# Transformer encoder trunk: the first stage rearranged (small inputs as rows, silu's row in PSUM, latent product behind the chunk loop)

## The chip, the cores and the metric

The kernel runs on one core of a Trainium2 chip. The metric is the device time of one execution in microseconds (us). Five engines work side by side, each through its own queue in order: TensorE (PE; its weight loads, PEld, overlap), VectorE (DVE), ScalarE (ACT), GpSimd (POOL) and SyncE (SP), which issues most DMAs. Operands lie in SBUF, matmul results in the eight banks of PSUM.

## The reference

Two layers of an encoder with hidden width 1024 on 512 positions. `c` goes through silu and one product per layer that gives shift, scale and gate for both halves of the layer.

```python
c_act = jax.nn.silu(c)
for l in range(DEPTH):
    mod = c_act @ w_mod[l] + b_mod[l]
    sh1, sc1, gt1, sh2, sc2, gt2 = jnp.split(mod, 6, axis=-1)
    h = rms_norm(x, g_norm_mix[l]) * (1.0 + sc1[:, None]) + sh1[:, None]
    proj = h @ w_in[l]
    q_d, k_d, v_d, cq, ckv, k_rope = jnp.split(proj, cuts, axis=-1)
    ...
    o_dil = dilated_attention(q_d, k_d, v_d, positions, slopes)
    o_mla = latent_attention(cq, ckv, k_rope, positions, ...)
    x = x + gt1[:, None] * (jnp.concatenate([o_dil, o_mla], -1) @ w_out[l])
    h = rms_norm(x, g_norm_mlp[l]) * (1.0 + sc2[:, None]) + sh2[:, None]
    x = x + gt2[:, None] * (jnp.square(jax.nn.relu(h @ w_mlp_in[l])) @ w_mlp_out[l])
```

The dilated heads subtract a slope times the distance of two positions; the latent heads turn part of q and k by sines and cosines of the positions.

## The kernel before, in words

x lies transposed, as eight tiles of 128 features by 512 positions (`xT`, chunk k or j). Every matrix product is made of three matmuls (`mm3`, lines 238 to 240): operands are split into a rounded part `hi` and the rest `lo`, and hi·hi, lo·hi and hi·lo are added in PSUM. A weight block is loaded as `raw` or `zz`, ACT makes `wh` and POOL makes `wl` (`load_split`, lines 233 and 234).

The first stage, up to the first head of attention, goes like this. Loads: c, the identity, the columns of small parameters (`cols`), positions as columns (`posc`), the rotary frequencies (`inv`), x. Silu of c is spread over all partitions as a row of 1024 (`cb`) by a product of ones with diagonal matrices. The squares of x are added up and summed over the features by a matmul (line 723). Sine and cosine of the angles are made on POOL and ACT (lines 131 to 151), with a table load on ACT ahead and one behind. Then comes the chunk loop (lines 720 to 750), k from -1 to 7: DVE multiplies two blocks of modulation weights (128 x 1024) by `cb` with a running sum (line 170), which gives shift and scale of a chunk; ACT makes `am` and `mod` of them (lines 195 and 194); DVE makes u, x times the inverse norm (lines 738 and 729); ACT makes `hi` and the full u (lines 742 and 743), and `lo` is made by POOL for even and by DVE for odd places (lines 745 and 733). With each chunk PE adds to four banks of the first dilated pair (`PR[0]`, 384 columns) and to four banks of the latent product (`W`, 416 columns).

Behind the loop come the norms of the dilated pair, its tail of 16 transposes (line 469), the norms and tail of the latent product (line 537), and the distances of the positions (`distances`, lines 304 to 325). Then eight head stages `st` follow, four of dilated pairs and four of latent pairs, each woven with the product of the next pair: a score (line 482), on DVE the bias and maximum (line 343), on ACT the exponential, a scaling on ACT or POOL, four transposes (line 358) and the product with the values (line 368).

The order on each engine is set by a scheduler that plays the program through. Instructions that are marked (`keep_in_program_order`, or issued inside `manual_schedule` for the listed engines) stay in the order of the code; the others are put where the scheduler sees room. Each tile name is a ring of buffers (`BUFS`: `qk` and `ot` 8, `raw` 3, `zz` 2, `wh`, `wl` and `mm` 4, `P` 3, `sc` and `tr` 2); a new tile waits until the readers of the one before it in its buffer are done.

Of the kernel before, what the change touches and what calls it, by code (L numbers as in the profile page):

```python
# [16 lines left out]
L = 2  # L17
D = 1024
# [24 lines left out]
def trunk(ctx: ExitStack, tc: tile.TileContext, a):  # L43
# [42 lines left out]
    cs = col(8, "cs")  # L86
    SY.dma_start(cs, a["c"].rearrange("(k p) -> p k", p=128))
    ident = const.tile([128, 128], F32, name="ident")
    SY.dma_start(ident, a["ident"])
    cols = [col(N_COL, f"cols{l}") for l in range(L)]  # L90
    SY.dma_start(cols[0], a["cols"][0])
    posc = const.tile([128, 4], I32, name="posc")
    SY.dma_start(posc, a["pos"].rearrange("(t p) -> p t", p=128))
    inv = col(16, "inv")
    SY.dma_start(inv, bass.AP(tensor=a["inv"].tensor, offset=a["inv"].offset, ap=[[0, 128], [1, 16]]))

    xT = [const.tile([128, S], F32, name=f"x{j}") for j in range(8)]
    for j in range(8):
        SY.dma_start(xT[j], a["xT"][j])
    ones = const.tile([128, 128], F32, name="ones")  # L100
# [3 lines left out]


    e = small(8)
    A.activation(e, cs, AF.Exp, scale=-1.0)
    V.tensor_scalar(e, e, 1.0, None, op0=OP.add)
    V.reciprocal(e, e)
    V.tensor_tensor(cs, cs, e, op=OP.mult)  # L110
    cb = const.tile([128, D], F32, name="cb")
    for i in range(2):
        p = ps("sc", (128, 4, 128))
        dg = s2([128, 4, 128])
        for k in range(4):
# [5 lines left out]
    sq0 = s2(tag="o")
    for j in range(8):
        if j == 0:
            A.activation(sq0, xT[j], AF.Square)
        else:
            sq = s2(tag="P")
            A.activation(sq, xT[j], AF.Square)
            V.tensor_tensor(sq0, sq0, sq, op=OP.add)


    pf = col(4, "pf")
    V.tensor_copy(pf, posc)
    ang, kf, w_ = s2([128, 4, 16]), s2([128, 4, 16]), s2([128, 4, 16], tag="b")
    for t in range(4):
        G.tensor_scalar(ang[:, t], inv, pf[:, t:t + 1], 0.0, op0=OP.mult, op1=OP.add)
    G.tensor_scalar(kf, ang, 1.0 / (2 * math.pi), 12582912.0, op0=OP.mult, op1=OP.add)
    G.tensor_scalar(kf, kf, -12582912.0, 0.0, op0=OP.add, op1=OP.add)
    c1 = 6.28125
    c2 = float(np.float32(np.round((2 * math.pi - c1) * 2.0 ** 20) / 2.0 ** 20))
    c3 = 2 * math.pi - c1 - c2  # L140
    for cc in (c1, c2, c3):
        G.tensor_scalar(w_, kf, -cc, 0.0, op0=OP.mult, op1=OP.add)
        G.tensor_tensor(ang, ang, w_, op=OP.add)
    PI_ = 3.1415925
    G.tensor_scalar(ang, ang, PI_, -PI_, op0=OP.min, op1=OP.max)
    A.activation(kf, ang, AF.Abs)
    G.tensor_scalar(kf, kf, -1.0, math.pi / 2, op0=OP.mult, op1=OP.add)
    sin = const.tile([128, 4, 16], F32, name="sin")
    cos = const.tile([128, 4, 16], F32, name="cos")
    A.activation(sin, ang, AF.Sin)  # L150
    A.activation(cos, kf, AF.Sin)
    pre = A.preload_act_table_set("natural_log_exp_and_others")
    tc.keep_in_program_order(pre)
    ctx.enter_context(tc.issue_after(pre.ins))
# [7 lines left out]
    def mod_block(l, i, tag="raw", pool_=False, pin=False, out=None):  # L162
        out = modc[l][:, i:i + 1] if out is None else out
        w = t4(tag, [128, D], F32)
        SY.dma_start(w, a["wmod"][l, i])
        if pool_:
            G.tensor_tensor(w, w, cb, op=OP.mult)
            A.activation(w, w, AF.Copy, accum_out=out)
        else:
            r = V.scalar_tensor_tensor(w, w, 1.0, cb, op0=OP.mult, op1=OP.mult, accum_out=out)  # L170
            if pin:
                tc.keep_in_program_order(r)
# [17 lines left out]
    mraw = col(16, "mraw")  # L190

    def first_norm(j):

        A.activation(modc[0][:, j:j + 1], mraw[:, j:j + 1], AF.Identity, bias=cols[0][:, C_BMOD + j:C_BMOD + j + 1])
        A.activation(amix[0][:, j:j + 1], mraw[:, 8 + j:9 + j], AF.Identity, bias=gb0[:, j:j + 1],
                     scale=cols[0][:, C_GMIX + j:C_GMIX + j + 1])

# [31 lines left out]
    def load_split(src, n, raw="raw", tags=("wh", "wl")):  # L229
        raw = t4(raw, [128, 1024], F32)[:, :n]  # L230
        hi, lo = t4(tags[0], [128, 1024])[:, :n], t4(tags[1], [128, 1024])[:, :n]
        SY.dma_start(raw, src)
        A.activation(hi, raw, AF.Copy)  # L233
        G.tensor_tensor(lo, raw, f(hi), op=OP.subtract)  # L234
        return hi, lo

    def mm3(out, sh, sl, mh, ml, first, last):
        T.matmul(out, sh, mh, start=first, stop=False)  # L238
# [5 lines left out]
    def inv_rms(p, v, y, t):  # L244

        V.tensor_scalar(v, p, 1.0 / D, EPS, op0=OP.mult, op1=OP.add)
        A.activation(t, v, AF.Ln)
# [3 lines left out]
        V.scalar_tensor_tensor(y, t, 1.5, p, op0=OP.add, op1=OP.mult)  # L251
# [719 lines left out]
```

## Time and profile before

| | |
|---|---|
| three runs | 1353.58, 1353.67, 1356.93 us; median 1353.67 |
| the profiled execution | 1351.23 us |
| its span, first to last instruction | 1349.5 us |
| busy: PE, PEld | 1271.8 us (94%), 1116.2 us (83%) |
| busy: DVE, ACT, POOL | 761.6 (56%), 680.4 (50%), 653.0 us (48%) |
| mean granted clock of TensorE | 0.973 of full speed |

A row of the timeline has the start in us, the busy time, engine, source line, operation, tile written and tiles read; x4 says that four instructions are merged. A bracket at the end gives the idle time of the engine ahead of it and what ended it. A name such as `h` or `mm` is that of the tile, without its buffer number. PEq, SPq and the like are an engine's queue.

### The profile page before, as it was taken

What the parts mean: (1) busy time and instruction counts of PE and PEld (TensorE: products, weight loads), DVE (VectorE), ACT (ScalarE), POOL (GpSimd) and SP (SyncE); (2) the same over time, 40 slices, a digit from 0 to 9 for tenths busy, and PEclk for the clock granted to TensorE, in tenths of its full rate; (3) what the DMA queues carried; (4) which work ended last, traced back from release to release, by engine and by line L of the source; (5) the groups of instructions that cost most, each with busy time, mean ns of one, the idle gap of its engine ahead of it and who ended that gap; (6) DMA issues with size and microseconds to landing.
All of it is one profiled execution on the core that took longest, in us unless ns stands there. A gap on an engine that the chain in (4) does not pass through costs nothing.

```text
span 1349.5 us, 19637 instructions
## 1 busy us (share of the span) xinstructions
PE 1271.8 (94%) x7114; PEld 1116.2 (83%) x7114; DVE 761.6 (56%) x1644; ACT 680.4 (50%) x1421; POOL 653.0 (48%) x504
## 2 busy tenths in 40 slices
PE   4889989898999999999999999899799999999999
PEld 2778867777998888888899999798699888888888
DVE  6777787875763561834576678987573122121123
ACT  5567898776542332322247677887653232232321
POOL 5636786674445444444438333545443444444441
PEclk6979989999999999999999999999999999999999
DMA  9335543341244572754534243211111322233221
GB/s 343 113 102 173 182 155 103 105 134 62 71 164 165 185 266 94 266 172 157 167 122 129 79 136 123 85 48 63 60 51 54 103 94 94 94 99 104 94 94 63
DMA packets 57248, 167.62 MB, mean 124 GB/s; under 512 B 8640, under 2 KB 10816, under 8 KB 57152
## 3 DMA queue, kind: packets, MB, share of 16 engines
q1 hardware_dynamic: 57152, 166.38, 37.5%
q8 instruction: 56, 0.92, 0.3%
q14 instruction: 40, 0.33, 0.1%
HBM read 155.87 MB, written 10.49 MB: 123 GB/s over the span
## 4 chain that ended last, share of the span: by engine, by line
PE 66%; POOL 2%; DVE 2%; ACT 2%; issue 2%; DMA 1%; POOLq 0%; DVEq 0%; ACTq 0%
PE mm L240 20%; PE mm L238 20%; PE mm L239 20%; PE tr L368 2%; PE tr L358 1%; POOL wl L234 1%; PE sc L238 1%; PE sc L239 1%; PE sc L240 1%; POOL pt L234 1%; PE sc L482 0%; PE mm L469 0%; DVE pt L362 0%; PE sc L483 0%; PE mm L626 0%
## 5 line engine op out<-in xcount | busy, mean ns | idle before, releaser
L234 POOL TENSOR_TENSOR wl<-raw,wh 128x1024 fp32r<-128x1024 f32 (+3 forms) x174 | 395.7, 2276 | 440.1 <-ACT wh L233 436.4
L233 ACT ACTIVATE wh<-raw 128x1024 fp32r<-128x1024 f32 (+3 forms) x174 | 174.6, 1004 | 263.9 <-PE mm L240 211.7
L659 DVE SCALAR_TENSOR_TENSOR x<-mm,mod,x 128x512 f32<-128x512 f32 (+1 forms) x152 | 92.4, 620 | 255.7 <-PE mm L240 255.2
L238 PE MATMUL mm<-h,wh 128*128 128x512 f32 (+1 forms) x544 | 198.5, 365 | 0.2
L239 PE MATMUL mm<-h,wl 128*128 128x512 f32 (+1 forms) x544 | 198.1, 364 | 0.0
L240 PE MATMUL mm<-h,wh 128*128 128x512 f32 (+1 forms) x544 | 197.9, 364 | 0.0
L238 PE MATMUL mm<-ot,wh 128*128 128x512 f32 (+1 forms) x416 | 147.9, 357 | 7.3 <-ACT ot L651 5.2
L843 ACT ACTIVATE P<-mm 128x512 f32<-128x512 f32 (+1 forms) x80 | 41.1, 513 | 214.3 <-PE mm L240 208.2
L239 PE MATMUL mm<-ot,wl 128*128 128x512 f32 (+1 forms) x416 | 146.7, 354 | 0.0
L240 PE MATMUL mm<-ot,wh 128*128 128x512 f32 (+1 forms) x416 | 144.2, 354 | 2.2 <-POOL ot L652 2.2
L844 DVE SCALAR_TENSOR_TENSOR mm<-mm,P 128x512 f32<-128x512 f32 (+1 forms) x80 | 46.9, 589 | 132.1 <-ACT P L843 132.1
L238 PEld LDWEIGHTS mm<-h,wh 128*128 128x128 f32 x544 | 102.6, 189 | 16.8 <-DVE qk L846 0.6
L239 PEld LDWEIGHTS mm<-h,wl 128*128 128x128 f32 x544 | 102.7, 189 | 16.1
L240 PEld LDWEIGHTS mm<-h,wh 128*128 128x128 f32 x544 | 102.6, 189 | 16.2
L238 PE MATMUL mm<-qk,wh 128*128 128x512 f32 (+1 forms) x288 | 105.3, 366 | 1.0 <-DVE x L659 1.0
L239 PE MATMUL mm<-qk,wl 128*128 128x512 f32 (+1 forms) x288 | 105.3, 365 | 0.0
L240 PE MATMUL mm<-qk,wh 128*128 128x512 f32 (+1 forms) x288 | 105.2, 365 | 0.0
L170 DVE SCALAR_TENSOR_TENSOR pt<-pt,cb 128x1024 f32<-128x1024 f32 x56 | 100.6, 1828 | 0.0
L355 POOL TENSOR_SCALAR P<-P,hs 128x512 f32<-128x512 f32 x64 | 48.4, 756 | 106.0 <-DVE hs L348 85.2
L362 DVE TENSOR_TENSOR pt<-tr,pt 128x512 fp32r<-128x512 f32 x128 | 86.6, 683 | 19.1 <-ACT pt L361 18.5
L238 PEld LDWEIGHTS mm<-ot,wh 128*128 128x128 f32 x416 | 80.1, 193 | 19.2 <-ACT ot L651 5.7
L238 PE MATMUL mm<-wh,h 128*128 128x384 f32 x240 | 81.0, 352 | 11.8 <-ACT h L742 9.8
(290 smaller groups left out, 2980.2 us busy)
## 6 DMA issues: line engine op xcount, KB each, us to landing
raw<-in_w_dram SPq DMA_DIRECT2D x64, 512.0 KB, 3.4
pt<-in_wmod_dram SPq DMA_DIRECT2D x56, 512.0 KB, 4.8
raw<-in_w2a_dram SPq DMA_DIRECT2D x48, 512.0 KB, 3.5
raw<-in_wmod_dram SPq DMA_DIRECT2D x24, 512.0 KB, 3.6
raw<-in_win_dram SPq DMA_DIRECT2D x30, 384.0 KB, 3.1
bias<-b SPq DMA_DIRECT2D x32, 256.0 KB, 2.3
raw<-in_wout_dram SPq DMA_DIRECT2D x16, 512.0 KB, 3.7
raw<-in_w2b_dram SPq DMA_DIRECT2D x16, 512.0 KB, 3.4
```

The costliest lines, as they stand in the source:

```text
L170: r = V.scalar_tensor_tensor(w, w, 1.0, cb, op0=OP.mult, op1=OP.mult, accum_out=out)
L233: A.activation(hi, raw, AF.Copy)
L234: G.tensor_tensor(lo, raw, f(hi), op=OP.subtract)
L238: T.matmul(out, sh, mh, start=first, stop=False)
L239: T.matmul(out, sl, mh, start=False, stop=False)
L240: T.matmul(out, sh, ml, start=False, stop=last)
L355: G.tensor_scalar(P, P, r_, 0.0, op0=OP.mult, op1=OP.add)
L362: V.tensor_tensor(lo, tr, f(hi), op=OP.subtract)
L368: T.matmul(po[:, HALF[qh]], vals(hd, kc), pt[qh][w][:, kc], start=(kc == 0 and w == 0), stop=(kc == 3 and w == 1))
L659: V.scalar_tensor_tensor(xT[j][:, hf], p, gt[:, j:j + 1], xT[j][:, hf], op0=OP.mult, op1=OP.add)
L843: A.activation(r, p, AF.Relu)
L844: V.scalar_tensor_tensor(p, p, 0.0, r, op0=OP.max, op1=OP.mult)
```

## The change

- c and the positions are loaded as rows of contiguous elements and turned into columns by small transposes on PE. Positions, `inv` and `cols` are issued from ACT's queue, so SP has c, the identity and then x.
- Silu's row stays in two PSUM banks (`cbp`); the first 16 modulation products are done in halves of 512 columns against these banks, with two partial sums (`mraw`) that POOL adds (`msum`, `first_sums`). The copy `cb` is made later, for the other modulation blocks.
- All sixteen modulation loads use the eight `qk` buffers. SP loads modulation rows and the dilated weights in turn; the latent weights follow behind.
- The squares are added in a PSUM bank; sine and cosine are one activation, made behind the squares with the table loads around it; the cosine's argument is made on DVE.
- In the chunk loop PE works on the dilated pair only. All `lo` are made by POOL. The latent product follows in two parts of two blocks each, with the dilated tail between them.
- The distances are made on POOL and DVE behind the chunk loop and no longer behind the latent tail; the rope tables move into the second head stage.

The diff, cut to its core (removed lines that the listing above shows are left out):

```diff
...
+    rows = s2([8, 4, 128], tag="b")
+    crow, prow, pi = rows[:, 0], rows[:4, 1].bitcast(I32), rows[:4, 2:].bitcast(I32)
+    SY.dma_start(crow, a["c"].rearrange("(k p) -> k p", k=8))
     SY.dma_start(ident, a["ident"])
...
     for j in range(8):
         SY.dma_start(xT[j], a["xT"][j])
+    A.dma_start(prow, a["pos"].rearrange("(t p) -> t p", t=4))
+    A.dma_start(inv, bass.AP(tensor=a["inv"].tensor, offset=a["inv"].offset, ap=[[0, 128], [1, 16]]))
+    A.dma_start(cols[0], a["cols"][0])
...
+    exp_tables()
     e = small(8)
+    turn = ps("sc")
+    T.transpose(turn[:, :8], crow, ident[:8, :8])
+    A.activation(e, turn[:, :8], AF.Exp, scale=-1.0)
...
+    cbp = [ps("tr") for _ in range(2)]
     for i in range(2):
+        dg = s2([128, 4, 128], tag="P")
...
+        T.matmul(cbp[i], ones, dg.rearrange("p k c -> p (k c)"), start=True, stop=True)
...
+    def first_sums(j):
+        G.tensor_tensor(msum, mraw[:, 0, j:16:8], mraw[:, 1, j:16:8], op=OP.add)
 
     def first_norm(j):
+        A.activation(amix[0][:, j:j + 1], msum[:, 1:2], AF.Identity, bias=gb0[:, j:j + 1],
+                     scale=cols[0][:, C_GMIX + j:C_GMIX + j + 1])
+        A.activation(modc[0][:, j:j + 1], msum[:, 0:1], AF.Identity, bias=cols[0][:, C_BMOD + j:C_BMOD + j + 1])
...
         for qb in range(4):
             d = dist[qb // 2][:, qb % 2]
-            A.activation(d, row[:, 0], AF.Identity, bias=clm[:, 0, qb:qb + 1], scale=65536.0)
+            r = G.tensor_scalar(d, row[:, 0], 65536.0, clm[:, 0, qb:qb + 1], op0=OP.mult, op1=OP.add)
+            tc.keep_in_program_order(r)
...
+            def mods(k):
+                ml[8 + k] = mod_load(0, 8 + k, "qk")
+                ml[k] = mod_load(0, k, "qk")
...
+            def late_split(i):
+                W["put"](i, *split(wr[4 + i], 2 * W_C, ("ot", "ot") if i < 2 else ("wh", "wl")))
+            def mod_mul(i):
+                for w in range(2):
+                    c = slice(512 * w, 512 * w + 512)
+                    V.scalar_tensor_tensor(ml[i][:, c], ml[i][:, c], 1.0, cbp[w], op0=OP.mult, op1=OP.mult,
+                                           accum_out=mraw[:, w, i:i + 1])
...
+            with tc.manual_schedule(engines={E.SP, E.DVE, E.Activation, E.Pool}):
+                for k in range(8):
+                    mods(k)
+                    if k % 2 == 0:
+                        weights(k // 2)
+                for i in range(4):
+                    late(i)
+                rotary()
+                sq0, sqp = s2(tag="o"), ps("mm")
+                A.activation(sqp, xT[0], AF.Square)
+                for j in range(1, 8):
+                    sq = s2(tag="P")
+                    A.activation(sq, xT[j], AF.Square)
+                    V.tensor_tensor(sq0 if j == 7 else sqp, sqp, sq, op=OP.add)
+                T.matmul(p, ones, sq0, start=True, stop=True)
+                V.scalar_tensor_tensor(cos, sin, -1.0, sin, op0=OP.mult, op1=OP.min)
+                V.tensor_scalar(cos, cos, math.pi / 2, None, op0=OP.add)
+                A.activation(sines, sines, AF.Sin)
+                exp_tables()
+                banks = [ps("mm") for _ in range(4)]
+                mod_mul(8)
+                mod_mul(0)
+                first_sums(0)
+                PR[0]["put"](0, *split(wr[0], 768))
+                inv_rms(p, v, t)
+                for k in range(8):
...
+                    V.tensor_tensor(u, xT[k], p, op=OP.mult)
+                    first_norm(k)
+                    A.activation(hi, u, AF.Identity, bias=be, scale=ga)
+                    A.activation(u, u, AF.Identity, bias=be, scale=ga)
+                    G.tensor_tensor(lo, u, f(hi), op=OP.subtract)
+                    if k % 2 == 0 and k < 6:
+                        PR[0]["put"](k // 2 + 1, *split(wr[k // 2 + 1], 768))
+                    if k < 7:
+                        mod_mul(9 + k)
+                        mod_mul(k + 1)
+                        first_sums(k + 1)
+                    if k > 5:
+                        late_split(k - 6)
+                    for tb in range(4):
+                        PR[0]["step"](banks[tb][:, :384], k, tb)
...
+            lbanks = [ps("sc") for _ in range(2)]
+            for tb in range(2):
+                for k in range(8):
+                    W["step"](lbanks[tb][:, :W_C], k, tb, pin=tb == 0 and k == 0)
+            bias0 = distances(posr), g
             for fn in PR[0]["tail"]:
                 fn()
...
+            for tb in (2, 3):
+                lbanks.append(ps("mm"))
+                for k in range(8):
+                    W["step"](lbanks[tb][:, :W_C], k, tb)
+                W["do_chain"](tb, lbanks[tb])
...
+            if l == 0 and st == 1:
+                ev += [(2, W["rope"])]
```

Two places of the order show how instructions move. The first is POOL from the first weight split on. `raw`, `zz` and `wh` belong to weights, `pt` is u, `h` on the left is `lo`. Before:

```order
L234 TENSOR_TENSOR wl<-raw,wh 128x768
L234 TENSOR_TENSOR wl<-raw,wh 128x832
L234 TENSOR_TENSOR wl<-zz,wh 128x768
L234 TENSOR_TENSOR wl<-zz,wh 128x832
L745 TENSOR_TENSOR h<-pt,h 128x512
L234 TENSOR_TENSOR wl<-raw,wh 128x768
```

The same place now, with line 243 for the splits and 788 for `lo`, up to the fourth chunk's `lo`:

```order
L201 TENSOR_TENSOR msum<-mraw 128x2
L243 TENSOR_TENSOR wl<-raw,wh 128x768
L788 TENSOR_TENSOR h<-pt,h 128x512
L243 TENSOR_TENSOR wl<-zz,wh 128x768
L201 TENSOR_TENSOR msum<-mraw 128x2
L788 TENSOR_TENSOR h<-pt,h 128x512
L201 TENSOR_TENSOR msum<-mraw 128x2
L788 TENSOR_TENSOR h<-pt,h 128x512
L243 TENSOR_TENSOR wl<-raw,wh 128x768
L201 TENSOR_TENSOR msum<-mraw 128x2
L788 TENSOR_TENSOR h<-pt,h 128x512
```

Every chunk now has its `lo` on POOL, each `msum` stands behind the `lo` of the chunk before, and the second and third dilated split lie between such a `lo` and the next `msum` (the fourth does so two chunks on); the latent splits have left this place.

The second is PE at the end of the dilated product. `mm` with 384 columns are its banks, `sc` and `mm` with 416 the latent's. Before, in the loop's first chunk:

```order
L238 MATMUL mm49_202<-wh60_231,h31_184 128x384
L238 MATMUL mm50_203<-wh60_231,h31_184 128x384
L238 MATMUL mm51_204<-wh60_231,h31_184 128x384
L238 MATMUL mm52_205<-wh60_231,h31_184 128x384
L238 MATMUL sc53_206<-wh63_237,h31_184 128x416
L238 MATMUL sc54_207<-wh63_237,h31_184 128x416
L238 MATMUL tr55_208<-wh63_237,h31_184 128x416
L238 MATMUL tr56_209<-wh63_237,h31_184 128x416
```

Now, from the last matmuls of the second latent block on:

```order
L263 MATMUL sc113_543<-wh110_538,h30_157 128x416
L264 MATMUL sc113_543<-wl111_539,h29_156 128x416
L488 MATMUL mm117_607<-ident3_68,pt98_491 128x128 x4
L488 MATMUL mm118_614<-ident3_68,pt98_491 128x128 x4
L488 MATMUL mm119_621<-ident3_68,pt103_510 128x128 x4
L488 MATMUL mm120_628<-ident3_68,pt103_510 128x128 x4
L260 MATMUL mm136_678<-ot86_440,h23_150 128x416
L263 MATMUL mm136_678<-ot86_440,h24_151 128x416
```

The latent matmuls have left the chunk loop: two blocks stand behind it, then the dilated pair's 16 transposes, then the other two blocks, of which the first writes a bank of the ring that the transposes have just used.

More of the change, by code (lines that the diff above doesn't have):

```diff
@@ L121, in trunk @@
[L121 to L135, printed above, removed]
@@ new lines, in trunk @@
+    sines = const.tile([128, 2, 4, 16], F32, name="sines")
+    sin, cos = sines[:, 0], sines[:, 1]
+    clm = const.tile([128, 3, 4], F32, name="clm")
+    parts = s2([4, 3, 128], tag="b")
+    V.tensor_copy(parts[:, 2], prow)
+    V.tensor_scalar(pi[:, 0], prow, 16, None, op0=OP.arith_shift_right)
+    V.tensor_scalar(pi[:, 1], prow, 65535, None, op0=OP.bitwise_and)
+    V.tensor_copy(parts[:, :2], pi)
+    turn = ps("sc")
+    for i in range(3):
+        T.transpose(turn[:, 4 * i:4 * i + 4], parts[:, i], ident[:4, :4])
@@ new lines, in trunk, with rotary @@
+    V.tensor_copy(clm, turn[:, :12].rearrange("p (i t) -> p i t", i=3))
+    pf = clm[:, 2]
+    def rotary():
+        ang, kf, w_ = sin, cos, s2([128, 4, 16])
+        for t in range(4):
+            G.tensor_scalar(ang[:, t], inv, pf[:, t:t + 1], 0.0, op0=OP.mult, op1=OP.add)
+        G.tensor_scalar(kf, ang, 1.0 / (2 * math.pi), 12582912.0, op0=OP.mult, op1=OP.add)
+        G.tensor_scalar(kf, kf, -12582912.0, 0.0, op0=OP.add, op1=OP.add)
+        c1 = 6.28125
+        c2 = float(np.float32(np.round((2 * math.pi - c1) * 2.0 ** 20) / 2.0 ** 20))
+        c3 = 2 * math.pi - c1 - c2
+        for cc in (c1, c2, c3):
+            G.tensor_scalar(w_, kf, -cc, 0.0, op0=OP.mult, op1=OP.add)
+            G.tensor_tensor(ang, ang, w_, op=OP.add)
+        PI_ = 3.1415925
+        G.tensor_scalar(ang, ang, PI_, -PI_, op0=OP.min, op1=OP.max)
@@ L160, in trunk, with mod_load, mod_block @@
     amlp = [col(8, f"al{l}") for l in range(L)]
[L162 to L163 removed]
+    def mod_load(l, i, tag):
         w = t4(tag, [128, D], F32)
         SY.dma_start(w, a["wmod"][l, i])
+        return w
+    def mod_block(l, i, tag="raw", pool_=False, pin=False):
+        out = modc[l][:, i:i + 1]
+        w = mod_load(l, i, tag)
         if pool_:
@@ L424, in dil_prep @@
             w = dict(mm=[], chain=[])
-            w["load"], step = group(a["win"][l, pr], 384)
+            w["load"], step, w["put"] = group(a["win"][l, pr], 384)
             R = {}
@@ L511, in latent @@
             w = dict(mm=[], chain=[])
-            w["load"], step = group(a["winc"][l], W_C)
+            w["load"], step, w["put"] = group(a["winc"][l], W_C)
             def chain(tb, bank):
@@ L758, in trunk @@
+            bias0 = distances(posr), g
             for fn in PR[0]["tail"]:
                 fn()
+            for tb in range(2):
+                W["do_chain"](tb, lbanks[tb])
+            for i in range(2):
+                tc.keep_in_program_order(A.activation(cb[:, 512 * i:512 * i + 512], cbp[i], AF.Copy))
+            for i in range(2):
+                PR[1]["put"](i, *split(wr1[i], 768))
+            for tb in (2, 3):
+                lbanks.append(ps("mm"))
+                for k in range(8):
+                    W["step"](lbanks[tb][:, :W_C], k, tb)
+                W["do_chain"](tb, lbanks[tb])
```

187 lines of the change are left out of this document (69 added, 118 removed).

## The prediction

> **What bounds the kernel now.** I read the chain that ended last, then each engine's busy time by stretches of the program, and then the timelines of the first 120 us. The first row is the chain; in the others stand the stretch, its length, the busy time of PE, PEld, DVE, ACT and POOL, the granted clock, and the DMA share and rate.
>
> ```profile
> PE 66%; POOL 2%; DVE 2%; ACT 2%; issue 2%; DMA 1%; POOLq 0%; DVEq 0%; ACTq 0%
> ...
> 0.00:25.39 25.39, 5.45 (x6) 1.68 (x6) 14.74 (x43) 14.43 (x25) 11.89 (x20) 0.72 0.89 321
> 25.39:70.12 44.73, 39.72 (x192) 36.86 (x192) 33.69 (x46) 24.91 (x47) 28.85 (x23) 0.93 0.45 167
> 70.12:79.36 9.24, 4.59 (x20) 3.67 (x20) 7.93 (x22) 6.82 (x31) 3.30 (x2) 0.63 0.48 151
> 79.36:94.13 14.77, 12.81 (x58) 12.10 (x57) 11.85 (x30) 7.80 (x24) 3.31 (x6) 0.77 0.19 50
> ...
> 170.00:205.00 35.00, 27.61 (x168) 22.87 (x167) 29.96 (x82) 30.37 (x74) 28.94 (x29) 0.86 0.53 163
> ```
>
> The program as a whole hangs on PE (66% of the chain), but not at its beginning. Until 25.39 PE has 5.45 us of work: it waits for the first chunk of h. From 25.39 to 70.12 it runs the chunk loop, both products interleaved. From 70.12 to 79.36 it is busy for half the time at a clock of 0.63, waiting for the chain behind the first product, and up to 94.13 it waits and runs slowly again. All the changed code lies here. What PE gets done sooner here it keeps, as long as later stages wait for PE.
>
> **The change, part by part.** All instants are on the clock of the profile (span 1349.5 us, the execution itself 1351.23 us).
>
> *The wait for x.* Three small loads (cols, positions, inv) leave SP's queue, so x follows `ident` directly.
>
> ```profile
> 1.84 0.42 SPq L91 DMA_DIRECT2D cols<-in_cols_dram  x1
> ...
> 3.33 3.75 SPq L99 DMA_DIRECT2D x<-in_xT_dram  x8
> ...
> 6.72 0.63 ACT L124 ACTIVATE o<-x 128x512 f32<-128x512 f32 x1 [3.54 <-DMA x<-in_xT_dram]
> ...
> 9.06 4.72 DVE L128 TENSOR_TENSOR o<-o,P 128x512 f32<-128x512 f32 x6 [0.31 <-ACT P L127]
> ```
>
> x goes out at 1.84 in place of 3.33, 1.49 us sooner. The first square waits for x (its row says so), and the last add ended at 9.06 + 4.72 = 13.78; I let it end at 12.3. New waits could take this back: a squares' buffer is now shared with silu's diagonals, so ACT's squares wait for DVE's adds and for PE's product of silu, and behind them on ACT stand the table loads. So the gain lies between 0 and 1.49; I take 1.49, as the transfers still set the pace. The rows' transposes come beside this wait.
>
> *From the sum to the first chunk.* The rows are those of the steps before; all are on the way again, in another order, because sine and cosine now come after the squares.
>
> ```profile
> 15.44 1.28 ACT L150 ACT_TABLE_LOAD   x1
> 16.73 0.26 ACT L150 ACTIVATE sin<-s 128x64 f32<-128x64 f32 x1
> ...
> 17.16 1.28 ACT L152 ACT_TABLE_LOAD   x1
> ...
> 18.74 0.83 ACT L233 ACTIVATE wh<-raw 128x768 fp32r<-128x768 f32 x1
> ...
> 19.66 0.61 ACT L247 ACTIVATE b<-b 128x512 f32<-128x512 f32 x1
> ...
> 20.97 0.58 ACT L248 ACTIVATE sc<-b 128x512 f32<-128x512 f32 x1
> ...
> 21.63 0.69 DVE L249 TENSOR_TENSOR b<-b,sc 128x512 f32<-128x512 f32 x1 [4.81 <-ACT sc L248]
> ```
>
> After: two small DVE steps for the cosine (0.4 with hand-overs, an estimate by the 0.26 of a small activation), a table load 1.28, one activation for both 0.3, a table load 1.28, the split of the first weights 0.83, Ln 0.61, Exp 0.58, then on DVE three steps and u of chunk 0, 4 x 0.72 = 2.88, and on ACT `hi` and u, 2 x 0.82 = 1.64; with hand-overs 9.9. ACT's u of chunk 0 so ends at 12.3 + 9.9 = 22.2. The column-sum product on PE and the modulation of block 0 on DVE lie beside the table loads.
>
> *The chunk loop.* The next rows give count, shortest, median and longest duration in ns, and then single instructions.
>
> ```profile
> L195 ACT ACTIVATE am<-mraw,gb,cols x8: 370/386/388, 18.4 to 54.7; 128x1 f32<-128x1 f32 x8
> L194 ACT ACTIVATE mod<-mraw,cols x8: 278/294/298, 19.5 to 59.1; 128x1 f32<-128x1 f32 x8
> L742 ACT ACTIVATE h<-pt,mod,am x8: 812/816/820, 24.5 to 59.4; 128x512 fp32r<-128x512 f32 x8
> L743 ACT ACTIVATE pt<-pt,mod,am x8: 802/815/819, 25.4 to 60.3; 128x512 f32<-128x512 f32 x8
> ...
> 63.51 0.33 POOL L505 TENSOR_TENSOR rot<-sin,gr 128x64 f32<-128x64 f32 x1
> 63.80 1.85 POOL L234 TENSOR_TENSOR wl<-raw,wh 128x768 fp32r<-128x768 f32 x1
> 65.61 1.28 POOL L745 TENSOR_TENSOR h<-pt,h 128x512 fp32r<-128x512 f32 x1
> ...
> 32.07 2.27 POOL L745 TENSOR_TENSOR h<-pt,h 128x512 fp32r<-128x512 f32 x1
> ...
> L170 DVE SCALAR_TENSOR_TENSOR pt<-pt,cb x56: 1211/1802/2889, 385.8 to 689.8; 128x1024 f32<-128x1024 f32 x56
> L659 DVE SCALAR_TENSOR_TENSOR x<-mm,mod,x x152: 469/735/752, 233.8 to 1346.1; 128x512 f32<-128x512 f32 x80, 128x256 f32<-128x256 f32 x72
> ```
>
> Before, u of chunk 0 ended at 25.4 + 0.8 = 26.2 and that of chunk 7 at 60.3 + 0.8 = 61.1: 34.9 us for seven chunks. DVE made the pace, and its two-input products stretch beside POOL: L170 takes 1.21 at best and up to 2.89 us. The changed product reads silu's row from PSUM. No such product with accumulator is in the trace; the nearest, L659, reads PSUM and SBUF and never exceeds 0.75 us for 512 columns in 152 instances, while POOL worked half the time. DVE then needs 4 x 0.735 + 0.69 = 3.6 us a chunk, 25 us for seven.
>
> But the order shows a new serial chain through POOL. The sum `msum` of a chunk stands behind the `lo` of the chunk before, and `lo` behind ACT's u, which needs `msum`. One turn is msum 0.3 (bounds: nothing, and the 0.33 of 64 columns), am 0.39, mod 0.29, hi 0.82, u 0.82, lo 1.28: 3.90, with hand-overs 3.94. Where a split's `wl` stands between, 1.81 more: 5.75. The rows of the order put it into three of the seven turns (the latent splits stand behind `msum` and lie beside ACT): 3 x 5.75 + 4 x 3.94 = 33.0 us. DVE's 25 is the lower end; the upper has `lo` and `wl` stretched as in the row of 2.27 us, ten times 0.99 more, 42.9. I take 33.0, as the unstretched rows fit DVE's single SBUF input. u of chunk 7 ends at 55.2, six us sooner.
>
> *The latent product behind the loop.*
>
> ```profile
> 43.40 0.33 PE L240 MATMUL mm<-wl,h 128*128 128x384 f32 x1
> 43.58 0.33 PE L239 MATMUL mm<-wh,h 128*128 128x384 f32 x1
> ...
> 69.39 0.35 PE L240 MATMUL tr<-wl,h 128*128 128x416 f32 x1
> 69.58 0.35 PE L239 MATMUL tr<-wh,h 128*128 128x416 f32 x1
> ...
> 79.36 0.78 PE L482 MATMUL sc<-qk,qk 128*128 128x512 f32 x1
> ...
> 101.52 1.04 PE L469 MATMUL mm<-ident,zz 128*128 128x128 f32 x8
> ```
>
> Matmuls of 384 and 416 columns follow each other at 0.173 and 0.188 us. Behind u of chunk 7 come `lo` (1.3) and eight matmuls (1.4): the loop ends on PE at 58.0, where before it ended at 70.1 with both products done. The 48 latent matmuls of two blocks take 9.0 us, to 67.0, and cover the dilated product's chain, which before lay open in the 9.24 us behind 70.12. Sixteen transposes take 2.1; then a bank must come free through ACT and DVE, to 69.3; the other 48 take 9.0; the first score follows transposes at 78.8. Before it came at 79.36. So at this point only **0.6** of the six us is left: the rest went into latent work that used to lie inside the loop.
>
> *Behind the first score.* The first rows are windows of one clock period.
>
> ```profile
> 79.30:82.72 3.42, 3.42 (x12) 3.13 (x12) 3.12 (x15) 2.09 (x14) 0.00 (x0) 0.50 0.19 34
> 86.13:89.55 3.42, 1.46 (x11) 1.18 (x10) 1.91 (x4) 2.50 (x6) 0.00 (x0) 1.00 0.00 0
> 89.55:92.96 3.41, 3.41 (x12) 3.41 (x11) 3.41 (x6) 3.27 (x6) 0.59 (x1) 0.50 0.00 0
> 113.44:116.85 3.41, 1.63 (x10) 1.63 (x11) 3.31 (x9) 3.36 (x8) 3.41 (x3) 1.00 0.57 160
> ...
> 89.24 0.44 PE L238 MATMUL mm<-wh,h 128*128 128x384 f32 x1 [1.96 <-DVE ot L542]
> ...
> 94.13 0.68 DVE L343 CUSTOM_DVE_ANT_0 P<-sc,b 128x512 f32<-128x512 f32 x1
> ...
> 115.22 0.44 PE L469 MATMUL mm<-ident,zz 128*128 128x128 f32 x2 [2.09 <-DVE zz L459]
> ```
>
> Before, PE waits 1.96 us here and has two windows of 3.4 us at half clock, 1.7 lost in each: 5.4. After, the distances and biases are ready, the softmax starts at the first score instead of 94.13, and PE follows it: by the order four scores, the transposes of P and the latent's last transposes stand ahead of the next product, and between a score and its transposes lie DVE's 0.68, an exponential (about the 0.82 of a 512-wide step), a reciprocal (at most 0.33) and the scaling (about DVE's 0.7), 2.5 to 2.9 us; the other scores and small transposes fill some 0.8 of it: 2.0 of waiting. That wins **3.4**. Of the later 2.09 I count half, **1.1**, since the product and the heads are interleaved otherwise (bounds 0 and 2.1). The sum is 0.6 + 3.4 + 1.1 = **5.1 us**, 1346.1 against the execution's 1351.2; the median of the runs, 1353.67, is 2.4 above it, so 1348.6.
>
> *Costed at nothing:* the distances on POOL (before, it is busy for 3.30 of the 9.24 us there; without that cover four steps); rope's ten small steps, now in the second head stage, at 0.33 each; the modulation loads, now in eight buffers, of which the ninth waits for DVE's first product, with the weights queued behind it (the DMA share was 0.45 in the loop, DVE is ahead of POOL; without this cover each late load delays a turn); the late latent load that waits for POOL's last `wl`, with positions and the next weights behind it, under the 18 us of latent matmuls. The reordering in later stages may take or give a us or two; I give it none.
>
> *A rule against the trace.* In the rows above, the window that was 43% busy (1.46 of 3.42) was followed by half clock, that with 48% (1.63 of 3.41) was not. The changed loop gives PE 12 x 0.173 = 2.1 us a turn: 53% of a short turn, 36% of a long one. So I expect it to fall to half clock and recover; at half clock a turn takes 4.2, less than a long one. The Trainium skill ("TensorE: Matmul & The Clock Gate", "What's actually happening") has the clock fall only after an idle window of about 3.4 us. By that rule the loop would stay warm, since its gaps are about 2 us; the sum would not change. The trace disagrees: 43% busy was not enough.
>
> **Rivals.** *POOL is still stretched,* so the change does not do what it says: with `lo` and `wl` at the contended 2.27, the loop takes 9.9 us more, and the kernel is slower by 4.8, 1358.5. It turns slower from 0.51 us for each of the ten instructions. For it: the 2.27 row; against: L659.
> *The gain ends in the first head stage:* its heads and not PE set its end, so only 0.6 stays: 1353.1. For it: the row 170 to 205, where PE is busy for 27.6 of 35; against: the wait at 115.22 is for the next product's chain and for no head.
> *The clock:* PE comes cold out of the loop and falls again at the first score, two half-clock windows, 3.4 lost: 1352.0. For it: the 43% window; against: the last three turns are short.
> *The heads' lead pays too:* the softmax starts some 15 us sooner, and of the 7.4 us that PE idles from 170 to 205 five go as well: 10.1, 1343.6. For it: that row; against: PE's order is different there.
>
> **How the numbers follow.** Forecast 0.52, at 1348.6, with its own range of 1345.6 (all 5.4 behind the first score and all 2.09 won) to 1351.2 (nothing won from x's issue and from the 2.09); contention 0.09; heads 0.19; clock 0.10; lead 0.10. About 0.3%, or 4.1 us, is what a measurement of this kernel can tell from no change. Faster: 0.42 of the forecast and the lead, 0.52. Slower: 0.07 of the contention. Same: 0.41. The range of 1342.5 to 1354.5 reaches from the lead to the heads and leaves out the contention and the edges.
>
> **What the profile would show.** First x square near 5.2; ACT's first `hi` near 20.5 (before 24.5) and its last u ending near 55; POOL's `lo` at 1.28 throughout and turns of 3.9 and 5.8; PE's loop end near 58, first score near 79, the first softmax on DVE right behind it. The forecast is wrong if the loop runs at DVE's pace, if squares wait for buffers, or if later stages do not keep the lead.

## The result, and the profile after

The changed kernel takes 1369.57 us (median of 4 runs, 1366.45 to 1370.18) against 1353.62 us before in the same job. The ratio is 1.0112, with an interval of 1.0098 to 1.0125: it is 1.1% **slower**, where the forecast was 5 us faster, and the time lies above the range. The profiled execution is the fastest of the four, 1366.45 us with a span of 1364.3, 15.2 us above the profiled execution of before. All instants below are on the clocks of the two profiles.

The first rows are from the timelines of DVE and ACT in the changed kernel: start, duration, engine, line, output and inputs, and in brackets the wait just before and who ended it.

```profile
5.53 0.60 ACT L764 ACTIVATE mm<-x 128x512 f32<-128x512 f32 x1 [1.73 <-DMA x<-in_xT_dram]
...
5.74 0.17 DVE L195 SCALAR_TENSOR_TENSOR gb<-cols 128x8 f32<-128x8 f32 x1 [1.42 <-DMA cols<-in_cols_dram]
...
8.47 0.68 DVE L768 TENSOR_TENSOR mm<-mm,P 128x512 f32<-128x512 f32 x1
...
9.19 2.02 ACT L767 ACTIVATE P<-x 128x512 f32<-128x512 f32 x3 [2.33 <-DVE mm L768]
...
13.87 0.69 DVE L768 TENSOR_TENSOR o<-mm,P 128x512 f32<-128x512 f32 x1
...
20.09 0.60 ACT L272 ACTIVATE sc<-b 128x512 f32<-128x512 f32 x1 [0.76 <-DVE b L271]
```

The first square of x starts at 5.53 (6.72 before), but the last add of the squares ends at 14.56, later than before (13.78). DVE's first add stands at 8.47 behind silu's chain and the diagonals, and these stand behind `gb` on DVE, which waited for `cols` until 5.74. ACT's third square waits 2.33 us and starts as that first add ends; the squares go through `P`, a ring of three buffers that the diagonals use too.

The next rows group the chunk loop's instructions: count, shortest, median and longest duration in ns, first and last start in us.

```profile
L787 ACT ACTIVATE pt<-pt,mod,am x8: 812/814/818, 24.5 to 56.8; 128x512 f32<-128x512 f32 x8
L788 POOL TENSOR_TENSOR h<-pt,h x8: 1267/1272/1299, 25.4 to 57.7; 128x512 fp32r<-128x512 f32 x8
L750 DVE SCALAR_TENSOR_TENSOR qk<-qk,tr x32: 669/678/684, 14.8 to 43.8; 128x512 f32<-128x512 f32 x32
L201 POOL TENSOR_TENSOR msum<-mraw x8: 190/196/373, 17.4 to 54.9; 128x2 f32<-128x2 f32 x8
```

ACT's u of chunk 0 ends at 25.3 and that of chunk 7 at 57.6: 32.3 us for seven turns. `lo` takes 1.27 to 1.30 us in all eight chunks and DVE's product 0.67 to 0.68: nothing is stretched.

Behind the loop, these rows of PE's timeline are the first score and all the waits of over 0.5 us up to 120 us:

```profile
82.05 0.47 PE L501 MATMUL sc<-qk,qk 128*128 128x512 f32 x1
...
85.36 0.50 PE L501 MATMUL sc<-qk,qk 128*128 128x512 f32 x1 [0.96 <-DVE hs L360]
...
111.80 0.66 PE L375 MATMUL tr<-ident,P 128*128 128x128 f32 x4 [1.57 <-ACT P L368]
...
114.11 0.66 PE L375 MATMUL tr<-ident,P 128*128 128x128 f32 x4 [1.65 <-POOL P L372]
...
116.11 0.66 PE L488 MATMUL mm<-ident,zz 128*128 128x128 f32 x2 [1.35 <-DVE zz L478]
```

The first score comes at 82.05 (79.36 before). From there PE runs 28 us with one wait of 0.96 us. So far little is lost. The time is lost further on. The table gives the instant at which the last product with the values ends for some of the sixteen heads of the first layer (1 to 8 the dilated ones, two in each head stage, 9 to 16 the latent ones), read from PE's records, in us. The runs of the next section are in it too.

| kernel | first score | head 3 | head 4 | head 6 | head 8 | head 16 | span |
|---|---|---|---|---|---|---|---|
| before | 79.4 | 148.2 | 166.2 | 193.3 | 225.3 | 333.4 | 1349.5 |
| changed | 82.1 | 147.6 | 171.6 | 203.7 | 241.1 | 343.6 | 1364.3 |
| rope_tail | 82.4 | 148.1 | 167.5 | 200.7 | 231.7 | 339.6 | 1358.4 |
| rope_first_stage | 82.5 | 146.5 | 165.2 | 198.6 | 230.1 | 339.0 | 1358.3 |
| before_rope_late | 78.5 | 145.3 | 166.7 | 195.1 | 230.9 | 347.1 | 1366.5 |
| product_later | 82.3 | 148.1 | 166.2 | 197.2 | 235.2 | 339.0 | 1358.0 |
| product_on_pool | 83.9 | 149.7 | 169.1 | 196.9 | 238.8 | 345.0 | 1366.4 |
| before_product_later | 79.4 | 150.2 | 169.9 | 198.9 | 230.2 | 344.5 | 1360.3 |
| free_rope1 | 82.4 | 148.2 | 172.4 | 204.6 | 241.4 | 344.2 | 1363.1 |
| distances_late | 81.4 | 147.9 | 172.8 | 200.7 | 233.1 | 347.1 | 1366.2 |
| front_early | 80.9 | 146.9 | 171.3 | 203.5 | 240.4 | 346.1 | 1364.8 |
| three_undone | 82.6 | 147.5 | 161.7 | 193.9 | 229.1 | 336.7 | 1352.4 |
| front_three | 80.6 | 146.2 | 162.0 | 193.9 | 227.4 | 333.8 | 1351.4 |
| front_product | 80.9 | 146.5 | 162.3 | 197.6 | 226.1 | 337.4 | 1354.6 |

At the end of head 3 the changed kernel is 0.6 us ahead. At the end of head 4 it is 5.4 us late, at head 6 10.4, at head 8 15.8, and at head 16 10.2. Up to the last update of x in the first layer it becomes 11.5 (721.4 for 709.9), and the second layer adds 3.4 (642.9 us from there to the end, for 639.5).

What happens between heads 3 and 4 stands in the chain of waits of the changed kernel (start, duration, what):

```profile
143.80 1.31 POOL b L356
145.13 0.41 DVE P L360
145.55 3.22 DMA raw<-in_win_dram
...
149.66 0.60 ACT o L387
150.28 0.68 DVE o L388
151.04 0.62 DVE pt L379
151.66 5.58 DVE raw L176 x2
157.54 0.70 DVE zz L478
158.29 0.69 PE mm L488 x2
158.98 0.32 PE mm L260
```

A bias step on POOL, a softmax on DVE behind it, a load of weights, ACT's work behind the split that waits for that load, and then **5.58 us in one of DVE's modulation products** (L176), which mostly takes 1.22. PE stands behind it, and the windows show what follows (stretch, length, then busy time of PE, PEld, DVE, ACT and POOL, granted clock, DMA share and rate):

```profile
147.81:151.23 3.42, 0.43 (x4) 0.21 (x2) 1.64 (x5) 2.54 (x7) 3.42 (x5) 0.83 0.68 222
151.23:154.64 3.41, 1.76 (x8) 1.31 (x7) 3.41 (x2) 2.82 (x6) 3.41 (x3) 0.50 0.22 84
154.64:158.05 3.41, 0.00 (x0) 0.00 (x0) 3.38 (x6) 0.63 (x1) 1.51 (x2) 0.50 0.00 0
158.05:161.47 3.42, 3.18 (x11) 3.18 (x12) 1.98 (x4) 0.09 (x1) 0.00 (x0) 0.50 0.96 287
```

PE works for 0.43, 1.76 and 0.00 us of three windows of 3.4 us and then runs its next product at half clock, 0.32 us a matmul. POOL is busy without a gap from 140.77 until 156.15, and its timeline says with what. Two rows of SP's queue and one of ACT's stand among those of POOL:

```profile
139.38 0.63 ACT L355 ACTIVATE b<-ot 128x512 f32<-128x512 f32 x1
...
140.77 0.32 POOL L520 TENSOR_TENSOR rot<-sines,gr 128x64 f32<-128x64 f32 x1 [2.63 <-DMA gr<-in_gkr_dram]
...
142.25 1.30 POOL L524 TENSOR_TENSOR rot<-sines,gr 128x64 f32<-128x64 f32 x1
...
143.80 1.30 POOL L356 TENSOR_TENSOR b<-b,ot 128x512 f32<-128x512 f32 x1
...
145.13 0.33 SPq L357 DMA_DIRECT2D bias<-b  x1
145.55 2.66 SPq L251 DMA_DIRECT2D raw<-in_win_dram  x2
...
146.00 1.84 POOL L243 TENSOR_TENSOR wl<-raw,wh 128x768 fp32r<-128x768 f32 x1
...
151.34 3.59 POOL L243 TENSOR_TENSOR wl<-raw,wh 128x768 fp32r<-128x768 f32 x2
154.88 1.27 POOL L356 TENSOR_TENSOR b<-b,ot 128x512 f32<-128x512 f32 x1
```

L520 and L524 are two of rope's steps, which the change put here; L356 are bias steps of the softmax, L243 weight splits. Rope's two tables share one buffer `gr`, so the load for the second goes out when the first is done, at 136.92, and POOL, idle since 138.14, stands 2.63 us waiting for it with a bias step behind it in its queue. ACT had made that bias step's input by 140.00; it starts at 143.80, and the next one waits 5.2 us (in the kernel before, none of this stage waits over 1.9). The load of weights at 145.55 in turn stands on SP's queue behind the store of the late bias. From 151.34 to 156.15 two splits and a bias step run without a pause, and DVE's product, started at 151.58, ends 1.08 us after them. The waits of DVE from 140 to 160 us (who for whom, us in all, times, longest) have one row, where before had none on POOL's biases:

```profile
DVE P L360 <- POOL b L356: 3.7, 2, 2.2
```

PE's waits from 140 to 165 us in the changed kernel, and behind the dots those of before:

```profile
PE mm L488 <- DVE zz L478: 5.3, 1, 5.3
PE tr L375 <- DVE o L388: 3.0, 1, 3.0
PE tr L385 <- DVE pt L379: 1.3, 1, 1.3
...
PE sc L482 <- DVE hs L343: 1.8, 1, 1.8
PE mm L469 <- DVE zz L459: 0.2, 1, 0.2
```

### The profile page after: what moved, and what is told of

The parts are those of the page before. It is cut to its first block, busy times and chain, and to the rows that moved or that the text cites. A ratio compares the mean times of both kernels' runs of the same rounds, so it can differ in the third digit from the quotient of the medians.

```text
span 1364.3 us, 19700 instructions
## 1 busy us (share of the span) xinstructions
PE 1276.0 (94%) x7118; PEld 1120.1 (82%) x7118; DVE 754.7 (55%) x1675; ACT 677.9 (50%) x1415; POOL 643.8 (47%) x519
## 4 chain that ended last, share of the span: by engine, by line
PE 75%; ACT 7%; DVE 6%; POOL 5%; issue 3%; DMA 3%; ACTq 0%; SPq 0%; POOLq 0%; DVEq 0%
PE mm L264 22%; PE mm L260 22%; PE mm L263 21%; PE tr L385 3%; PE tr L375 2%; POOL wl L243 2%; ACT wh L242 1%; PE sc L260 1%; PE sc L263 1%; PE sc L264 1%; ACT pt L378 1%; DMA raw<-in_wout_dram 1%; ACT P L361 1%; DVE pt L379 1%; PE mm L647 1%
## 5 line engine op out<-in xcount | busy, mean ns | idle before, releaser
L243 POOL TENSOR_TENSOR wl<-raw,wh 128x1024 fp32r<-128x1024 f32 (+2 forms) x173 | 392.5, 2271 | 449.6 <-ACT wh L242 446.7
L242 ACT ACTIVATE wh<-raw 128x1024 fp32r<-128x1024 f32 (+2 forms) x173 | 173.8, 1006 | 265.8 <-PE mm L264 211.5
L260 PE MATMUL mm<-ot,wh 128*128 128x512 f32 (+1 forms) x416 | 147.9, 357 | 5.3 <-ACT ot L672 5.3
L375 PE MATMUL tr<-ident,P 128*128 128x128 f32 x512 | 79.0, 280 | 22.8 <-DVE o L388 7.9
L176 DVE SCALAR_TENSOR_TENSOR pt<-pt,cb 128x1024 f32<-128x1024 f32 x56 | 100.3, 1822 | 0.0
L260 PE MATMUL mm<-wh,h 128*128 128x384 f32 (+1 forms) x248 | 84.8, 360 | 11.1 <-ACT h L786 10.8
L263 PE MATMUL mm<-wh,h 128*128 128x384 f32 (+1 forms) x248 | 88.9, 359 | 6.5 <-POOL h L788 6.5
```

The costliest lines, as they stand in the source:

```text
L242: ra = A.activation(hi, raw, AF.Copy)
L243: rg = G.tensor_tensor(lo, raw, f(hi), op=OP.subtract)
L260: r = T.matmul(out, sh, mh, start=first, stop=False)
L263: T.matmul(out, sl, mh, start=False, stop=False)
L375: T.transpose(tr[:, kc], P[:, kc * 128:(kc + 1) * 128], ident)
```

## The experiments

Theory A was that rope's place makes the loss; A' that the product's stall does, and rope only sets the trap; B that the early heads meet the stage in a worse phase. Medians are of each run's executions; those of before lie between 1353.2 and 1354.8 us in the same jobs.

**Rope's place.** Rope's steps back behind the latent tail. There are fourteen of them, ten for the two tables and four on k (L520 to L524 twice, L570 to L573); the prediction and the expectations say ten.

```diff
             W["tail"]()
+            W["rope"]()
...
-            if l == 0 and st == 1:
-                ev += [(2, W["rope"])]
```

> The changed kernel with rope's ten steps back behind the latent tail, ahead of the heads. Theory A (rope's steps in the second head stage line POOL up, so that two weight splits and a bias step then run back to back, DVE's two-input product waits 5.65 us beside them, its buffer, the load behind it and PE's next weights come late): DVE's products stay at 1.2 to 2.3 us, PE keeps its weights at 140 to 165 us, and some 10 to 12 us come back, 1357 to 1360 us. Theory B (the heads start 11 us sooner and meet weights and products in a worse phase, whatever POOL does with rope): the idle time of PE from 145 to 160 us stays, 1367 to 1371 us.

Measured: 1361.12 us, ratio 1.0053 [1.0033, 1.0073], 8.5 less than the changed kernel. Of the products in that group none now takes over 2.87 us, and the waits of PE from 140 to 165 us are shorter:

```profile
L176 DVE SCALAR_TENSOR_TENSOR raw<-raw,cb x18: 1204/1218/2871, 94.6 to 296.2; 128x1024 f32<-128x1024 f32 x18
```

```profile
PE mm L488 <- DVE zz L478: 2.2, 1, 2.2
PE tr L375 <- DVE o L388: 2.0, 1, 2.0
PE tr L375 <- DVE pt L379: 0.8, 1, 0.8
```

Theory B's number is excluded; A's is met in size (1 us short of its range). What is left, 7.3 us, B could still explain.

The same steps one stage earlier:

```diff
-            if l == 0 and st == 1:
+            if l == 0 and st == 0:
                 ev += [(2, W["rope"])]
```

> The changed kernel with rope's ten steps one head stage earlier, in the first one, where POOL has a gap of some 10 us (96.8 to 107.5 us on its timeline) and no weight split waits. Theory A (rope is only dear where POOL's splits already queue): as in the run rope_tail, 1359 to 1362 us. Rival (rope costs wherever it stands among heads): 1366 to 1371 us.

Measured: 1361.96 us, 1.0053 [1.0035, 1.0071]. Among the first stage's heads rope costs no more than ahead of them all: the second stage is the wrong place, not the heads as such.

The same move alone, in the kernel before (the steps split off the tail, held in order, called at due time 2 of the second stage):

```diff
+            def rope():
                 lat["Cq"], lat["Sq"] = rope_tables(a["gqr"][l], 0)
...
+            if l == 0 and st == 1:
+                ev += [(2, W["rope"])]
```

> The kernel before with nothing but rope's ten steps moved into the second head stage, held in program order as in the change. Theory A: this alone costs 8 to 12 us, 1361 to 1366 us. Theory A' (it needs the product and the splits to meet, which depends on the heads' phase): within 3 us of before, or a loss wherever they meet. Theory B: no change, 1351 to 1356 us.

Measured: 1366.97 us, 1.0091 [1.0068, 1.0114]: 13.1 us lost by this edit alone, more than A said, and near the whole loss of the change (in the two profiles 2.8 lie in the second layer, whose steps are held here too: from the last update of x in the first layer to the end 642.3 us against 639.5). But not where A said: head 4 ends 0.5 us late, head 8 5.6, head 16 13.7, and no such product is longer than 2.41 us. The edit is dear in either kernel; the 5.6 us stall is only one of the ways in which it is paid.

**The product.** The stalled one moved to the fourth head stage:

```diff
+                if st == 1:
+                    on_dve = ("MV0", "MV1", "MV3")
+                elif st == 3:
+                    on_dve = ("MV2",)
```

> The changed kernel with one modulation product of the second head stage (the one that took 5.65 us on DVE) done in the fourth stage instead; rope stays where the change put it. Theory A': the product's wait is the cause of the loss, rope only sets the trap: the stall is gone and 8 to 12 us come back, 1358 to 1362 us. Theory A (POOL itself is late in that stage by rope's steps, the product only shows it): at most 4 us come back, 1365 to 1369. Theory B: no change, 1367 to 1371 us.

Measured: 1358.95 us, 1.0042 [1.0025, 1.0058], 10.6 less than the changed kernel: A', not A. Head 4 ends at 166.2, as before; 6 us are lost again from head 6 to head 8, in the stage that got the product: 38.0 us between the two ends, against 32.0 before. The product is not shown to be the reason: the changed kernel, which has none there, takes 37.4, and before_product_later (next), which has it there, 31.3.

The same edit in the kernel before:

> A control: the kernel before, with the same product moved from the second to the fourth head stage. If the product hurts only where the change has lined POOL up against it: 1352 to 1356 us, as before. If moving it is a gain of its own, whatever the change: 1344 to 1349 us.

Measured: 1360.91 us, 1.0058 [1.0042, 1.0074]: neither. The edit that gains 10.6 us in the one kernel costs 7.7 in the other. Neither expectation had allowed for a loss.

The product left at its place, but computed on POOL, its sum on ACT:

```diff
-                ev += [(tn(x), lambda: next_mod(pin=True)) for x in on_dve]
+                ev += [(tn(x), lambda x=x: next_mod(pool_=True) if st == 1 and x == "MV2" else next_mod(pin=True)) for x in on_dve]
```

> The changed kernel with rope where the change put it and the one product of the second head stage at its place, but computed on POOL (about 2.2 us there) with its sum on ACT, so that DVE holds no two-input product there. If DVE standing blocked for 5.65 us is the price: PE's wait of 5.3 us for DVE's normalized rows goes and 6 to 10 us come back, 1359 to 1364 us, though POOL has more to do. If POOL's own backlog or the buffer and the load behind the product are the price: 1367 to 1373 us.

Measured: 1366.02 us, 1.0078 [1.006, 1.0096], between the two. PE's waits from 140 to 165 us are now these two alone, the 5.3 us for `zz` is gone:

```profile
PE tr L375 <- DVE o L388: 3.3, 1, 3.3
PE tr L385 <- DVE pt L379: 1.3, 1, 1.3
```

Head 6 ends at 196.9, 6.8 us sooner than in the changed kernel; by head 8 only 2.3 of them are left. So the blocked DVE did cost some 7 us, and the stages behind it took back two thirds.

**The second layer.** Rope's steps of the second layer not held in order:

```diff
+            pinned = tc.keep_in_program_order if l == 0 else (lambda i: i)
...
-            tc.keep_in_program_order(G.tensor_tensor(C[:, :, 0], cos, ga, op=OP.mult))
...
+            pinned(G.tensor_tensor(C[:, :, 0], cos, ga, op=OP.mult))
```

> The changed kernel with rope's steps of the second layer left to the scheduler, as before the change; the first layer's stay as changed. Theory P (the 3.4 us that go from the heads of the second layer, between 870 and 985 us, come from the order that these eight held steps force on POOL and on all that is planned behind them): 1365 to 1367 us and the second layer's POOL order as before. Theory Q (the second layer's loss is follow-up noise of its start 12 us later): 1368 to 1371 us.

Measured: 1364.99 us, 1.0081 [1.0064, 1.0099], 4.6 less by the medians: theory P. By the spans of the single profiles, which scatter, it is 1.2 us. The second layer alone tells more: from the last update of x in the first layer to the end, the two kernels in which these steps were never held and the four in which they were set free (this one and the last three runs below) take 639.3 to 640.6 us, the eight in which they are held 640.9 to 643.1.

**The front.** The small DVE steps on `cols` behind the sum of squares:

```diff
-    V.scalar_tensor_tensor(gb0, cols[0][:, C_BMOD + 8:C_BMOD + 16], 1.0, cols[0][:, C_GMIX:C_GMIX + 8], op0=OP.add, op1=OP.mult)
...
+                V.scalar_tensor_tensor(gb0, cols[0][:, C_BMOD + 8:C_BMOD + 16], 1.0, cols[0][:, C_GMIX:C_GMIX + 8], op0=OP.add, op1=OP.mult)
                 mod_mul(8)
...
+                gains()
                 posr = s2([128, S], I32)
...
-            gains()
```

> The changed kernel with the five small DVE steps on the cols (gains and gb) moved behind the sum of squares, so that silu's chain and the diagonals, and with them the first add, no longer wait for cols: the first add near 7 us in place of 8.5, the last near 12 in place of 14.6, ACT's first h near 21 in place of 23.7, the first score near 79.5 in place of 82.1. If a gain at the front reaches the end: 1366 to 1367 us. If it ends in the first head stages, where the heads and the weight loads set the end: 1368.5 to 1370.5 us.

Measured: 1365.82 us, 1.008 [1.005, 1.0109]. DVE's timeline, with the first five and the last of the adds behind the diagonals:

```profile
6.86 0.70 DVE L767 TENSOR_TENSOR mm<-mm,P 128x512 f32<-128x512 f32 x1 [0.29 <-ACT P L766]
8.25 3.92 DVE L767 TENSOR_TENSOR mm<-mm,P 128x512 f32<-128x512 f32 x5 [0.69 <-ACT P L766]
12.27 0.69 DVE L767 TENSOR_TENSOR o<-mm,P 128x512 f32<-128x512 f32 x1
```

The last add ends at 12.96, 1.6 us sooner than in the changed kernel, ACT's first `h` comes at 22.1 (23.7) and the first score at 80.9 (82.1): half of what was expected at the first score. The median is 3.75 us lower, but this run's single profile has a span 0.5 us above the changed kernel's, and the interval is 4 us wide on either side. That such a gain reaches the end is likely, not shown.

The distances behind the latent tail, with rope there too, to be compared with rope_tail:

```diff
-            bias0 = distances(posr), g
             for fn in PR[0]["tail"]:
...
             W["tail"]()
+            W["rope"]()
+            bias0 = distances(posr), g
```

> The changed kernel with rope in the tail (as in the run rope_tail, 1361.1 us) and the distances behind the latent tail too, so that the first heads start about where they did before. Theory B' (what is left of the loss without rope, some 7 us, comes from heads that start 11 us early and then meet the weights of the second stage late): the first softmax back near 92 us and 1353 to 1357 us. Theory D (the early heads are a gain of some 3 us as predicted, and the rest of the loss has another cause): 1361 to 1365 us.

Measured: 1369.54 us, 1.0117 [1.0087, 1.0147], 8.4 more than rope_tail: theory B' falls, since heads that start later (head 1 ends at 111.7, in the changed kernel at 103.6) make it worse. D said 1361 to 1365, so it falls in size as well. Head 3 ends as in rope_tail (147.9 and 148.1), head 4 5.3 us later.

**Together.** The three repairs (rope in the tail, the product later, the second layer free):

> The changed kernel with all three steps taken back that each gave time alone: rope behind the latent tail, one product of the second head stage moved to the fourth, rope's steps of the second layer left to the scheduler. If rope and the product are two ends of one stall in the second head stage, they give together little more than the 10.6 us of the product alone, and the second layer's 4.6 us come on top: 1353 to 1357 us. If they are separate losses, 8.5 + 10.6 + 4.6 us come back: 1345 to 1348 us, faster than before.

Measured: 1356.39 us, 1.0015 [1.0003, 1.0027], 13.2 less than the changed kernel. Singly they gave 8.5, 10.6 and 4.6, or 23.7. That fits the theory by which rope and product are two ends of one stall.

With the front's edit as well:

> The run three_undone (1356.4 us) with the five small DVE steps behind the sum of squares as in front_early. If the front's gain of 3.7 us and the second stage's repairs are independent: 1352 to 1353.5 us. If the front's gain is eaten again by the fourth head stage, where three_undone lost 5 to 6 us: 1355 to 1358 us.

Measured: 1354.8 us, 1.0013 [0.9999, 1.0027], between the two ranges and nearer to the one by which the gain is eaten. It can't be told from before.

And with the product put at the end of the chunk loop instead of the fourth stage:

```diff
+                ml[16] = mod_load(0, 16, "qk")
...
+                    V.scalar_tensor_tensor(ml[16][:, c], ml[16][:, c], 1.0, cbp[w], op0=OP.mult, op1=OP.mult,
+                                           accum_out=m16[:, w:w + 1])
+                V.tensor_tensor(modc[0][:, 16:17], m16[:, 0:1], m16[:, 1:2], op=OP.add)
+                modq.pop(0)
```

> As front_three, but the product taken out of the second head stage goes to no other stage: it is done at the end of the chunk loop, where DVE is idle for 8 us, from the two PSUM banks, with one more 512 KB load into a buffer that is free by then. Theory (a two-input product costs what the stage it stands in has to wait for; in the fourth stage it cost the 4.7 us by which the heads' ends moved there): 1346 to 1350 us, faster than before. Rival (every new order of the head stages costs some us, whatever stands in them): 1353 to 1360 us.

Measured: 1354.6 us, 1.001 [1.0001, 1.0019]: the rival. Head 4 ends 3.9 us ahead of before and head 6 4.3 behind it, though no head stage has got anything more to do. No run beat the kernel before.

## Why the prediction was wrong

**The wait for x:** forecast 1.49 us won, measured 0.8 lost. The square did come sooner (5.53). The step priced the add by the pace of the transfers. The risk that it named and set at nothing, a squares' buffer, came in: the third square waited 2.33 us. What it did not see is why: silu's diagonals stand ahead of the first add on DVE, and `cols`, now third on ACT's queue, ahead of those. front_early shows it: with this order undone 1.6 us come back, and the third square waits 0.77.

**From the sum to the first chunk:** forecast 9.9 us, measured 14.56 to 25.33 = 10.8. The row at 20.09 has most of it: Exp writes the bank that DVE's step on the variance reads, and waits 0.76 us for it.

**The chunk loop:** forecast 33.0 us with turns of 5.75 and 3.94, measured 32.3 with three of 5.6 and four of 3.8 to 4.0. The serial chain through POOL, and the product that no longer shares DVE's inputs with it, were both right. The rival of a stretched POOL is refuted for the loop.

**The latent product and the first score:** forecast 78.8, measured 82.05. Of these 3.25 us, u of chunk 0 is late by 3.1 (25.3 for 22.2); the loop is 0.7 shorter, and the work behind it 0.8 longer (24.4 us from u of chunk 7 to the score, for 23.6). That the last two nearly cancel is luck.

**Behind the first score:** forecast 4.5 us won by the end of head 3 (3.4 and 1.1), measured 3.3: 2.7 late at the first score, 0.6 ahead at head 3. Up to 115.9 us PE did stay at full clock and waited 0.96 us, but three waits of 1.35 to 1.65 us stand at the end of the first stage, and the granted clock of 116.85 to 120.26 was 0.64. Of the lead of 5.1 us, 0.6 was there.

**What failed** is the sentence on the edits costed at nothing: "rope's ten small steps, now in the second head stage, at 0.33 each", and the one behind it, that the reordering in later stages "may take or give a us or two; I give it none". Rope's place costs 8.5 us in this kernel, and the held steps in the second layer 4.6 by the medians; both together cost 13.1 in the kernel before. The prediction priced the steps by their own durations (and counted ten of fourteen). It named no work that hides them, nor what is queued behind them: POOL's bias steps, which here started up to 5.2 us late and for which DVE's softmax and SP's loads wait, and its splits, behind which DVE's product stood for 5.65 us. It also overlooked the load between rope's two tables, for which POOL stood 2.63 us; what that wait alone costs no run shows. POOL's busy share was on record: its own row for 170 to 205 us has 28.94 of 35 us, and the second head stage, from 134.65 to 170 us of the kernel before, 27.53 of 35.35.

**The rivals:** "the gain ends in the first head stage" was right for 110 to 120 us and blind to what follows. The rival on the slower side had put POOL's contention into the loop; it came in the second head stage, against DVE. The clock fell and recovered in the loop as forecast: it was full in the first of these windows, in which PE was busy for 1.39 of 3.41 us, and half in the next.

```profile
37.41:40.82 3.41, 1.39 (x7) 0.75 (x5) 3.41 (x12) 2.20 (x4) 1.03 (x3) 1.00 0.79 316
40.82:44.24 3.42, 2.48 (x8) 2.48 (x9) 3.42 (x10) 2.27 (x5) 1.04 (x2) 0.50 0.00 0
```

In that first window PE's longest wait was 1.73 us, so the Trainium skill's rule that the prediction weighed ("TensorE: Matmul & The Clock Gate", "What's actually happening"), by which the clock falls only after an idle window of about 3.4 us, is contradicted here too. Nor does a share of about 45% divide the cases, as the prediction's two windows suggest: in the kernel before, the window from 191.95 us, with PE busy for 1.84 of 3.41 us (54%) and the clock full, was followed by half clock.

**What stays open:** why the stages behind the stall lose what was won. Of the orders that were run, each loses somewhere between head 4 and the end, at another place each time. Which instruction decides it in the fourth stage and beyond was not traced. Nor does any run part what the moved steps cost by themselves from what any shift of a planned order costs: moving one product cost the kernel before 7.7 us, and moving the distances cost rope_tail 8.4. So 8.5 and 10.6 us are the prices of these edits in this order. A fourth buffer for the weights, which would have parted the late load from the late product, was not tried.

## What to carry to other kernels

A step moved into a busy stage is priced by what is queued behind it on its engine and by who waits for that, not by its own duration; ask for the busy share of that engine in that stage first, for what the step itself must wait for, and for when the inputs of the steps behind it are ready. Read the lead at several marks up to the end: the kernel was 0.6 us ahead at the end of head 3 and 5.4 late one head further. Where an order was planned around the exact instants of loads and products, any shift of one of them has to be run, since the same edit gained 10.6 us in one kernel and lost 7.7 in the other.

## What the runs showed of the hardware

DVE's product of two SBUF inputs usually waits for the POOL instruction under way and no longer: 2.40 us where 1.32 of POOL's lay ahead (changed kernel, 470.46 us), and 1.21 alone. In the changed kernel it waited for three in a row, 5.65 us, and at the same place in free_rope1 5.58 (second row) and in front_early 5.61:

```profile
L176 DVE SCALAR_TENSOR_TENSOR raw<-raw,cb x18: 1207/1216/5649, 94.2 to 304.9; 128x1024 f32<-128x1024 f32 x18
L176 DVE SCALAR_TENSOR_TENSOR raw<-raw,cb x18: 1205/1216/5576, 94.5 to 305.3; 128x1024 f32<-128x1024 f32 x18
```

The Trainium skill ("SBUF — State Buffer", "SBUF: two separate sides") has it that DVE and POOL share a pair of ports as an exclusive lock, which whichever starts first holds for its whole instruction. The usual cases agree; that two later POOL instructions went ahead of a waiting DVE is not in that rule, and no run here shows what decides it.
